# Handing GpSimd's 128x512 and larger work in the first attention to VectorE, and transposing a norm's column without widening it first

## The chip, the cores and the metric

One core of a Trainium2 chip runs the whole program. The metric is the device time of one execution in microseconds. TensorE (PE) does the matmuls, ScalarE (ACT) casts, exponentials and copies, VectorE (DVE) elementwise arithmetic and row maxima, GpSimd (POOL) elementwise arithmetic out of SBUF alone, SyncE (SP) issues the DMAs of the weights. Each engine works through its own queue in order.

## What is computed

A decoder trunk of two layers on 512 tokens of 1024 features, all in float32. The first layer has differential attention with 8 heads (two softmax maps per head, the second subtracted with a factor), the second one latent attention with 8 heads; each is followed by a squared-ReLU MLP. Cut to what matters here:

```python
def rms_norm(x, g, eps=EPS):
    return x * lax.rsqrt(jnp.mean(x * x, axis=-1, keepdims=True) + eps) * g

def apply_rope(x, cos, sin):
    x1, x2 = x[..., :half], x[..., half:]
    return jnp.concatenate([x1 * c - x2 * s, x2 * c + x1 * s], axis=-1)

def diff_attention(hn, ...):
    q, k, v = jnp.split(hn @ w_qkv, ...)
    q, k = apply_rope(q, cos, sin), apply_rope(k, cos, sin)
    s = einsum(q, k) * scale, causal
    p = softmax(s)
    a = p[:, :, 0] - lam * p[:, :, 1]
    o = rms_norm(a @ v, subln_g) * (1 - lambda_init)
    return o @ w_o
...
h = h + diff_attention(rms_norm(h, g0), ...);  h = h + sq_relu_mlp(rms_norm(h, g1))
k_nope, k_rope, v = mla_shared_kv(h, ...)
h = h + mla_attention(rms_norm(h, g2), ...);   h = h + sq_relu_mlp(rms_norm(h, g3))
return rms_norm(h, g_final)
```

## The kernel before

Activations lie with features on the 128 partitions and the 512 tokens along the row. Each float32 product is made of three matmuls on rounded parts (L341 to L353): a value is split into a high part `h`, a cast by ACT, and the rest `l`, a subtraction. For activations the subtraction is VectorE's. For weights, `Weights.prep` (L104 to L115) issues the subtraction (L113) on an engine that is chosen per weight tile; `W_E` is that engine for the weights of both attentions, and `FIRST_E` and `FIRST_BE` choose for the first six and the first four tiles of each. Before, all of the attentions' weight differences but those few are GpSimd's. A weight tile is 128x1024; four raw tiles are loaded ahead, and a raw tile's slot takes its next DMA when its subtraction is done.

`rope` (L485 to L511) rotates a head's queries or keys: ACT copies four swapped blocks of 32 rows from PSUM to `sw` (L492), VectorE multiplies the PSUM row with the cosines into `t` (L499), then `ROPE_E` multiplies `sw` with the sines (L495, called `q0sw` for the queries of head 0) and adds it to `t` (L501, `q0t`). Before, both of these are GpSimd's. Then `stack_q` (L455, L456) or `stack_k` (L470 to L472) make casts on ACT and differences on VectorE: `q0s`, `k0d` and `krest`. The scores of a head need all of them.

The norms' factors are columns: four numbers per partition, one for each 128 tokens. `rsqrt_cols` and L600 make them with a power on GpSimd. Where a factor is needed along the row, `row_wide` (L319 to L323) has VectorE copy the column out to 128x512 (tiles that end in `_w`), and `row_ps` (L325 to L329) has TensorE transpose the four blocks of it into PSUM. This is done for the first norm (the rotation's tables `tac`, `tas` are multiplied by it), for each of the 8 heads of the first attention, and three times ahead of the second (`rbB`, `lq`, `lc`).

The first attention runs tasks of one head and 128 queries: scores into PSUM, masked row maximum on VectorE (`a0..st`), exponential on ACT, the softmax factor `f` (L579, L580), the difference of the two maps (L581), transposes on TensorE, then `ath` (ACT) and `atl` (VectorE, L548), then the product with the values (`a0o`). Other projections fill the time between by a plan of lags (`LAG_A`, `LAG_N`). From the recorded operations a list scheduler puts each engine's instructions in order, by priorities and its own estimates; only at the start and at the very end is the program's order kept.

Of the kernel before, what the change touches and what calls it, by code (L numbers as in the profile page):

```python
# [15 lines left out]
P = 128  # L16
T = 512
NT = T // P
# [207 lines left out]
POOL, DVE = (lambda nc: nc.gpsimd), (lambda nc: nc.vector)  # L226
# [8 lines left out]
AT_C = (29.0, 30.5)  # L235


ROPE_E = (POOL, POOL)
W_E = POOL
FIRST_E = (DVE, DVE, DVE, POOL, DVE, POOL)  # L240
FIRST_BE = (DVE, DVE, DVE, POOL)
LAT_E = (DVE, DVE)


# [10 lines left out]
LAG_N = (2, 2, 4, 1)  # L255
# [6 lines left out]
def trunk(ctx: ExitStack, tc: tile.TileContext, io: dict, out: bass.AP):  # L262
    nc = Engines(tc)
# [10 lines left out]
    def big(name, dt=F32):  # L274
        return ap.tile([P, T], dt, name=name, tag="big", bufs=NBIG)

    def small(name, n=8):
        return ap.tile([P, n], F32, name=name, tag="small", bufs=48)

    def bank(name, tag):  # L280
        return ps.tile([P, T], F32, name=name, tag=tag, bufs=BANKS[tag])
# [33 lines left out]
    def transposes(dst, src_of, n=NT):  # L315
        for i in range(n):
            nc.tensor.transpose(dst[:, i * P:(i + 1) * P], src_of(i), ident)

    def row_wide(cols, name):  # L319
        wide = big(name + "_w")  # L320
        nc.vector.tensor_copy(wide.rearrange("p (i q) -> p i q", q=P),
                              cols.unsqueeze(2).to_broadcast([P, NT, P]))
        return wide  # L323

    def row_ps(wide, name):  # L325

        dst = bank(name + "_ps", "tr")
        transposes(dst, lambda i: wide[:, i * P:(i + 1) * P])
        return dst  # L329

    def split_into(h, l, src, scale=None):
# [8 lines left out]
    def split(src, name, scale=None, tiles=None):  # L340
        h, l = tiles or (big(name + "h", F32R), big(name + "l", F32R))  # L341
        split_into(h, l, src, scale)
        return h, l
# [135 lines left out]
    def mm2(dst, q, k, rest, tok, n, start):  # L479

        nc.tensor.matmul(dst, q[:, tok], k[:, :n], start=start, stop=False)
        nc.tensor.matmul(dst, q[:, tok], rest[:, :n], start=False, stop=True)
        later.spent(2 * PASS * max(256, n))

    def rope(src, tabs, got, name, parts=plain):  # L485
# [8 lines left out]
        def turn():  # L494
            ROPE_E[0](nc).tensor_mul(sw, sw, sinr)  # L495

# [63 lines left out]
    def task_a(hd, i, heads):  # L560

        name, n, tok = hd.name, P * (i + 1), slice(i * P, (i + 1) * P)
        qt = hd.quarter
        weave.need(lambda: len(qt.qs) > hd.hh and len(qt.ks) > hd.hh)
        q, k = qt.qs[hd.hh], qt.ks[hd.hh]
        if i == 0:
            hd.z = small(name + "z", 4)
        z0, z1 = hd.z[:, i:i + 1], small(name + "z1", 1)
        got = []
        for c in range(2):  # L570
            s = bank(f"{name}s{i}{c}", "s")
            mm2(s[:, :n], q[c], k[0][c], k[1][c], tok, n, True)
            got.append(softmax_parts(s, i, SCALE_A, (z0, z1)[c], f"{name}{i}{c}"))
        if i == NT - 1:
            keys_read.add(hd.at)
        yield from wait(LAG_A[1])
        p0, p1 = got
        f = small(name + "f", 1)
        nc.vector.reciprocal(f, z1)  # L579
        nc.vector.tensor_scalar(f, f, z0, nlam, op0=ALU.mult, op1=ALU.mult)  # L580
        nc.vector.scalar_tensor_tensor(p0[:, :n], p1[:, :n], f, p0[:, :n], op0=ALU.mult, op1=ALU.add)  # L581
        yield from wait(LAG_A[2])
        yield from attend(hd, p0, i, LAG_A[3])
        if i < NT - 1:
            return
        yield from wait(LAG_N[0])
        osb = big(name + "osb")
        nc.scalar.copy(osb, hd.o)
        yield from wait(LAG_N[1])
        otok = bank(name + "otok", "tr")  # L590
        transposes(otok, lambda j: osb[:, j * P:(j + 1) * P])
        ss, r = small(name + "ss", 4), small(name + "r", 4)
        junk = big(name + "junk")
        for j in range(NT):
            cols = slice(j * P, (j + 1) * P)
            nc.scalar.activation(junk[:, cols], otok[:, cols], AF.Square, accum_out=ss[:, j:j + 1])
        e = small(name + "e", 4)
        nc.vector.scalar_tensor_tensor(e, hd.z, SUBLN_EPS, hd.z, op0=ALU.mult, op1=ALU.mult)
        nc.vector.scalar_tensor_tensor(e, ss, 1.0 / P, e, op0=ALU.mult, op1=ALU.add)
        nc.gpsimd.tensor_tensor(r, e, mhalf.to_broadcast([P, 4]), op=ALU.pow)  # L600
        yield from wait(LAG_N[2])
        wide = row_wide(r, name + "rb")
        yield from wait(LAG_N[3])
        rbo = row_ps(wide, name + "rb")
        nc.vector.scalar_tensor_tensor(osb, osb, gsub, rbo, op0=ALU.mult, op1=ALU.mult)
        heads[hd.at] = split(osb, name + "on")

# [34 lines left out]
    rt, heads_a, heads_b = [], [None] * NH, [None] * NH  # L642
    r0 = small("r0", 4)
# [19 lines left out]
    ssq_m0, ssq_b, ssq_m1 = [], [], []  # L663
    W.eng = W_E(nc)
    quarters_a = [Quarter() for _ in range(4)]
# [3 lines left out]
    for n in ORDER_A:  # L669
        fill_a += qk_jobs(n) if n < NH else [v_job(n - NH)]  # L670
    for u, e in enumerate(FIRST_E):
        W.specs[u] = W.specs[u][:-1] + (e(nc),)
# [43 lines left out]
    krs, tkq = [], {}  # L716
# [226 lines left out]
    def turn_x(i):  # L943

        tok = slice(i * P, (i + 1) * P)
        trs = [bank(f"xT{i}{n}", "s" if i % 2 else "tr") for n in range(2)]
        for n in range(2):
            transposes(trs[n], lambda c: xt[i][n][:, c * P:(c + 1) * P])
        yield
        tr4 = [t.rearrange("p (c q) -> p c q", q=P) for t in trs]  # L950
        x4 = [big(f"x32{i}{n}").rearrange("p (c q) -> p c q", q=P) for n in range(2)]
        for n in range(2):
            gains = gcol[:, G_ATTN_A + 4 * n:G_ATTN_A + 4 * n + 4]
            nc.vector.tensor_mul(x4[n], tr4[n], gains.unsqueeze(2).to_broadcast([P, 4, P]))
        if i == 0:
            W.prep_h(1)
        else:
            nc.vector.tensor_copy(res[:, 0:4, tok], tr4[0])
        for n in range(2):
            nc.scalar.copy(xa[n][0][:, :, tok], x4[n])  # L960
        if i == 0:
            W.prep(1)
        for n, eng in enumerate((nc.gpsimd, nc.vector) if i == 0 else (nc.vector, nc.gpsimd)):
            h, l = xa[n]
            eng.tensor_sub(l[:, :, tok], x4[n], h[:, :, tok].bitcast(F32))
        if i == 0:
            nc.vector.tensor_copy(res[:, 0:4, tok], tr4[0])
            W.prep(2)
        nc.scalar.copy(res[:, 4:8, tok], tr4[1])
        yield  # L970
# [26 lines left out]
    sum_x(3)  # L997
    fill.pull(v_tile)
    gain_cols(grow_rest, G_ROWS - 16, 16)
    wide = row_wide(r0, "rb0")  # L1000


    lprod = const.tile([P, 2, HD], F32, name="lprod")
# [10 lines left out]
    fill.pull(v_tile)  # L1014
    nc.kept = False
    fill.pull(AT_TABLES)
    rt += tables(row_ps(wide, "rb0"), "ta")
    fill.drain()


# [39 lines left out]
    rB, r2B = small("rB", 4), small("r2B", 4)  # L1060
# [3 lines left out]
    def scale_b():  # L1064
        s = small("bssc", 4)
        col_sums(ssq_b[0], s, "csb")
        rsqrt_cols(rB, s, EPS, 1.0 / D)
        nc.vector.tensor_mul(r2B, rB, rB)
        w = row_wide(rB, "rbB")
        yield  # L1070
        tkq["k"] = tables(row_ps(w, "rbB"), "tk")

    def latent(raw, to, ssq, n, name):

        t, r = small(name + "s", 4), small(name + "r", 4)
        col_sums(ssq[0], t, name + "cs")
        nc.vector.tensor_mul(t, t, r2B)
        rsqrt_cols(r, t, EPS, 1.0 / n)
        nc.vector.tensor_mul(r, r, rB)
        w = row_wide(r, name + "rb")  # L1080
        yield
        row = big(name + "rbs")
        nc.scalar.copy(row, row_ps(w, name + "rb"))
        for m, x in enumerate(raw):
            LAT_E[0](nc).tensor_mul(x, x, row)
            to.append(split(x, f"{name}{m}", tiles=spare_pairs.pop(0) if spare_pairs else None))
# [81 lines left out]
```

## Time and profile before

| | |
|---|---|
| median of 3 runs | 1169.61 us (1167.59 to 1169.77) |
| the profiled execution | 1170.93 us, its span 1169.1 us |
| TensorE busy | 97% |
| VectorE, ACT, GpSimd busy | 53%, 46%, 19% |
| transposed start and first projections | 0 to 38 us |
| first attention | 38 to 260 us |
| first MLP | 260 to 630 us |
| second attention with its projections | 630 to 790 us |
| second MLP, final norm | 790 to 1169 us |

The times are those of one execution, from the start of its span. "Busy" counts an instruction from its start to its end, also where it stands still in between. [...] Waits are read from the view of who waited for whom, by stage.

### The profile page before, as it was taken

What the parts mean: (1) busy time and instruction counts of PE and PEld (TensorE: products, weight loads), DVE (VectorE), ACT (ScalarE), POOL (GpSimd) and SP (SyncE); (2) the same over time, 40 slices, a digit from 0 to 9 for tenths busy, and PEclk for the clock granted to TensorE, in tenths of its full rate; (3) what the DMA queues carried; (4) which work ended last, traced back from release to release, by engine and by line L of the source; (5) the groups of instructions that cost most, each with busy time, mean ns of one, the idle gap of its engine ahead of it and who ended that gap; (6) DMA issues with size and microseconds to landing.
All of it is one profiled execution on the core that took longest, in us unless ns stands there. A gap on an engine that the chain in (4) does not pass through costs nothing.

```text
span 1169.1 us, 14216 instructions
## 1 busy us (share of the span) xinstructions
PE 1137.7 (97%) x5528; PEld 951.8 (81%) x5528; DVE 625.4 (53%) x1035; ACT 541.2 (46%) x984; POOL 217.2 (19%) x144
## 2 busy tenths in 40 slices
PE   7899999999999999999999999999999999999996
PEld 7678888778888888888888789888888888888885
DVE  5677777867643334443555678755444233444232
ACT  6778777655442122442333577635443121443132
POOL 4665544312000100000111242304000000000011
PEclk9899999899999999999999999999999999999999
DMA  7321211213332333333322221123322333332311
GB/s 232 92 72 55 73 55 55 73 37 108 102 96 91 95 103 91 107 91 92 105 92 86 77 72 38 55 71 92 90 91 90 99 100 91 104 94 90 107 56 72
DMA packets 98319, 102.06 MB, mean 87 GB/s; under 512 B 4894, under 2 KB 86476, under 8 KB 98252
## 3 DMA queue, kind: packets, MB, share of 16 engines
q1 hardware_dynamic: 97532, 100.04, 27.8%
q8 instruction: 43, 0.70, 0.3%
q10 hardware_dynamic: 720, 1.11, 0.3%
q14 instruction: 24, 0.20, 0.1%
HBM read 99.05 MB, written 2.10 MB: 87 GB/s over the span
## 4 chain that ended last, share of the span: by engine, by line
PE 82%; ACT 7%; DVE 6%; issue 3%; POOL 1%; DMA 0%; POOLq 0%; SPq 0%; ACTq 0%; DVEq 0%
PE m0d L349 5%; PE m0d L350 5%; PE m0d L348 5%; PE m1u L348 5%; PE m1u L350 5%; PE m0u L348 5%; PE m0u L349 5%; PE m0u L350 5%; PE m1u L349 5%; PE m1d L350 4%; PE m1d L348 4%; PE m1d L349 4%; PE m1d L50 3%; PE ob L348 1%; PE ob L349 1%
## 5 line engine op out<-in xcount | busy, mean ns | idle before, releaser
L854 POOL TENSOR_TENSOR rt<-rt,gfin 128x512 f32<-128x512 f32 x4 | 5.2, 1297 | 301.3 <-ACT fjunk L852 301.1
L348 PE MATMUL m1u<-xn1h,m1u_4h 128*128 128x512 f32 x128 | 50.3, 393 | 0.0
L348 PE MATMUL m1u<-xn0h,m1u_0h 128*128 128x512 f32 x128 | 50.2, 392 | 0.0
L350 PE MATMUL m1u<-xn1h,m1u_4l 128*128 128x512 f32 x128 | 49.9, 390 | 0.0
L350 PE MATMUL m1u<-xn0h,m1u_0l 128*128 128x512 f32 x128 | 49.9, 390 | 0.0
L350 PE MATMUL m0u<-xm1h,m0u_4l 128*128 128x512 f32 x128 | 49.8, 389 | 0.0
L350 PE MATMUL m0u<-xm0h,m0u_0l 128*128 128x512 f32 x128 | 49.8, 389 | 0.0
L349 PE MATMUL m0u<-xm0l,m0u_0h 128*128 128x512 f32 x128 | 49.8, 389 | 0.0
L349 PE MATMUL m0u<-xm1l,m0u_4h 128*128 128x512 f32 x128 | 49.8, 389 | 0.0
L348 PE MATMUL m0u<-xm1h,m0u_4h 128*128 128x512 f32 x128 | 49.8, 389 | 0.0
L349 PE MATMUL m1u<-xn0l,m1u_0h 128*128 128x512 f32 x128 | 49.8, 389 | 0.0
L348 PE MATMUL m0u<-xm0h,m0u_0h 128*128 128x512 f32 x128 | 49.8, 389 | 0.0
L349 PE MATMUL m1u<-xn1l,m1u_4h 128*128 128x512 f32 x128 | 49.8, 389 | 0.0
L365 POOL TENSOR_TENSOR ssq_b<-ssq_b,sq 128x512 f32<-128x512 f32 x7 | 11.7, 1667 | 168.7 <-ACT sq L364 168.7
L695 POOL TENSOR_TENSOR res<-res,m0t 128x512 f32<-128x512 f32 x8 | 10.3, 1290 | 160.7 <-DVE m0t L694 160.7
L113 DVE TENSOR_TENSOR m1u_4l<-m1u_4r,m1u_4h 128x1024 fp32r<-128x1024 f32 x16 | 19.6, 1226 | 36.5 <-ACT m1u_4h L101 36.4
L113 DVE TENSOR_TENSOR m0u_4l<-m0u_4r,m0u_4h 128x1024 fp32r<-128x1024 f32 x16 | 19.9, 1245 | 32.5 <-ACT m0u_4h L101 32.4
L685 DVE TENSOR_TENSOR m1a<-m1u,m1a 128x512 f32<-128x512 f32 x32 | 22.0, 688 | 21.7 <-ACT m1a L684 21.7
L101 ACT CAST m1u_4h<-m1u_4r 128x1024 fp32r<-128x1024 f32 x16 | 16.8, 1050 | 34.7 <-PE m1u L349 21.6
L684 ACT ACTIVATE m0a<-m0u 128x512 f32<-128x512 f32 x32 | 19.0, 594 | 29.7 <-PE m0u L350 29.7
L685 DVE TENSOR_TENSOR m0a<-m0u,m0a 128x512 f32<-128x512 f32 x32 | 22.0, 686 | 19.0 <-ACT m0a L684 19.0
L365 POOL TENSOR_TENSOR ssq_m<-ssq_m,sq 128x512 f32<-128x512 f32 x14 | 20.9, 1494 | 59.0 <-ACT sq L364 58.9
(2301 smaller groups left out, 3720.4 us busy)
## 6 DMA issues: line engine op xcount, KB each, us to landing
m0u_0r<-in_w_up SPq DMA_DIRECT2D x16, 512.0 KB, 3.7
m0u_4r<-in_w_up SPq DMA_DIRECT2D x16, 512.0 KB, 3.7
m1u_0r<-in_w_up SPq DMA_DIRECT2D x16, 512.0 KB, 3.7
m1u_4r<-in_w_up SPq DMA_DIRECT2D x16, 512.0 KB, 3.7
wq_0r<-in_w_qkv_a SPq DMA_DIRECT2D x8, 512.0 KB, 4.9
wk_0r<-in_w_qkv_a SPq DMA_DIRECT2D x8, 512.0 KB, 4.2
xt<-in_x SPq DMA_DIRECT2D x8, 256.0 KB, 5.8
wv_0r<-in_w_qkv_a SPq DMA_DIRECT2D x4, 512.0 KB, 4.5
```

The costliest lines, as they stand in the source:

```text
L50: return self.owner.tc.keep_in_program_order(op(*args, **kw))
L101: self.nc.scalar.copy(d(h), v(self.raws[n]))
L113: eng.tensor_sub(d(to), v(self.raws[n]), d(h).bitcast(F32))
L348: nc.tensor.matmul(dst, ah, bh, start=start, stop=False)
L349: nc.tensor.matmul(dst, ah, bl, start=False, stop=False)
L350: nc.tensor.matmul(dst, al, bh, start=False, stop=stop)
L365: eng(nc).tensor_add(accum, accum, sq)
L684: nc.scalar.activation(a, dst, AF.Relu)
L685: nc.vector.tensor_mul(a, dst, a)
L695: (nc.gpsimd if half == 0 else nc.vector).tensor_add(res[:, c, :], res[:, c, :], t)
L854: nc.gpsimd.tensor_mul(t, t, gfin[0][:, :T])
```

## The change

Four tables change the engine of instructions. `ROPE_E` and `W_E` become VectorE, `FIRST_E` and `FIRST_BE` become empty, and the differences of the input's halves at the start are all VectorE's. `row_wide` goes: the transposes read the column itself with step 0, 128 times per block. GpSimd keeps the small powers and its sums in the MLPs. The lag that stood between the copy and the transposes of a head is kept as one sum.

```diff
-ROPE_E = (POOL, POOL)
-W_E = POOL
-FIRST_E = (DVE, DVE, DVE, POOL, DVE, POOL)
-FIRST_BE = (DVE, DVE, DVE, POOL)
+ROPE_E = (DVE, DVE)
+W_E = DVE
+FIRST_E = ()
+FIRST_BE = ()
...
-    def row_wide(cols, name):
-        wide = big(name + "_w")
-        nc.vector.tensor_copy(wide.rearrange("p (i q) -> p i q", q=P),
-                              cols.unsqueeze(2).to_broadcast([P, NT, P]))
-        return wide
-
-    def row_ps(wide, name):
+    def row_ps(cols, name):
 
         dst = bank(name + "_ps", "tr")
-        transposes(dst, lambda i: wide[:, i * P:(i + 1) * P])
+        transposes(dst, lambda i: cols[:, i:i + 1].to_broadcast([P, P]))
...
-        yield from wait(LAG_N[2])
-        wide = row_wide(r, name + "rb")
-        yield from wait(LAG_N[3])
-        rbo = row_ps(wide, name + "rb")
+        yield from wait(LAG_N[2] + LAG_N[3])
+        rbo = row_ps(r, name + "rb")
...
-        for n, eng in enumerate((nc.gpsimd, nc.vector) if i == 0 else (nc.vector, nc.gpsimd)):
+        for n, eng in enumerate((nc.vector, nc.vector)):
```

The same step from `row_wide` to `row_ps` of the column is made for `r0`, `rB` and the two latents' factors.

VectorE's queue at the keys of head 0, before, from the first product of `k0` to the two differences that its scores need:

```order
L499 TENSOR_TENSOR k0t<-k_0_435,tac 128x512
L456 TENSOR_TENSOR q0s_506<-q0t,q0s_506 64x512
L456 TENSOR_TENSOR q0s_507<-q0t,q0s_507 64x512
L499 TENSOR_TENSOR q1t<-q_0_474,tac 128x512
L472 TENSOR_TENSOR krest_67<-k0t,k0d_552 64x512
L472 TENSOR_TENSOR krest_68<-k0t,k0d_553 64x512
```

VectorE's queue at the same place now, from the sum of the queries' rotation on:

```order
L495 TENSOR_TENSOR q0t<-q0t,q0sw 128x512
L493 TENSOR_TENSOR k0t<-k_0_433,tac 128x512
L113 TENSOR_TENSOR wq_0l<-wq_0r,wq_0h 128x1024
L450 TENSOR_TENSOR q0s_504<-q0t,q0s_504 64x512
L489 TENSOR_TENSOR k0sw<-k0sw,tas 128x512
L450 TENSOR_TENSOR q0s_505<-q0t,q0s_505 64x512
L495 TENSOR_TENSOR k0t<-k0t,k0sw 128x512
L113 TENSOR_TENSOR wk_0l<-wk_0r,wk_0h 128x1024
L493 TENSOR_TENSOR q1t<-q_0_472,tac 128x512
L466 TENSOR_TENSOR krest_67<-k0t,k0d_550 64x512
L489 TENSOR_TENSOR q1sw<-q1sw,tas 128x512
L466 TENSOR_TENSOR krest_68<-k0t,k0d_551 64x512
```

Two weight differences and four rotation steps that were GpSimd's now stand among VectorE's own.

VectorE's queue at the third task of head 0, before, from its second maximum to the `atl` that the next product waits for:

```order
L525 ISA a021sm,a021st<-a0s_738,mask 128x384
L525 ISA a021st 128x1
L548 TENSOR_TENSOR a0atl_724<-a0tr_725,a0ath_723 128x128
L579 RECIPROCAL a0f<-a0z_729 128x1
L580 TENSOR_SCALAR a0f<-a0f,a0z,nlam 128x1
L581 SCALAR_TENSOR_TENSOR a020sm<-a021sm,a0f,a020sm 128x384
L456 TENSOR_TENSOR q2s_751<-q2t,q2s_751 64x512
L456 TENSOR_TENSOR q2s_752<-q2t,q2s_752 64x512
L548 TENSOR_TENSOR a0atl_724<-a0tr_770,a0ath_723 128x2x128
```

VectorE's queue there now:

```order
L519 ISA a021sm,a021st<-a0s_736,mask 128x384
L519 ISA a021st 128x1
L113 TENSOR_TENSOR wq_0l<-wq_0r,wq_0h 128x1024
L542 TENSOR_TENSOR a0atl_722<-a0tr_723,a0ath_721 128x128
L489 TENSOR_TENSOR k2sw<-k2sw,tas 128x512
L573 RECIPROCAL a0f<-a0z_727 128x1
L450 TENSOR_TENSOR q2s_749<-q2t,q2s_749 64x512
L450 TENSOR_TENSOR q2s_750<-q2t,q2s_750 64x512
L574 TENSOR_SCALAR a0f<-a0f,a0z,nlam 128x1
L542 TENSOR_TENSOR a0atl_722<-a0tr_768,a0ath_721 128x2x128
```

A weight difference and a rotation product come ahead of the reciprocal, and the difference of the maps moves behind the `atl`.

VectorE's queue ahead of the second attention, before, where the latent's factor `lcr` is made wide and the latent is scaled (`lat`) and split (`krest`, `lc1l`); `kr` is the rotary key:

```order
L312 TENSOR_SCALAR rs_e<-lcs 128x4
L1079 TENSOR_TENSOR lcr<-lcr,rB 128x4
L113 TENSOR_TENSOR wuq1l<-wuq1r,wuq1h 128x3x256
L321 COPY lcrb_w<-lcr 128x512
L113 TENSOR_TENSOR wuq1l<-wuq1r,wuq1h 128x3x128
L734 TENSOR_TENSOR kr<-kr_ps,krlo 64x512
L499 TENSOR_TENSOR krt<-kr,tkc 128x512
L1085 TENSOR_TENSOR lat_5572<-lat_5572,lcrbs 128x512
L1085 TENSOR_TENSOR lat_5587<-lat_5587,lcrbs 128x512
L335 TENSOR_TENSOR krest_74<-lat_5572,krest_73 128x512
L335 TENSOR_TENSOR lc1l<-lat_5587,lc1h 128x512
```

VectorE's queue there now:

```order
L312 TENSOR_SCALAR rs_e<-lcs 128x4
L726 TENSOR_TENSOR kr<-kr_ps,krlo 64x512
L1069 TENSOR_TENSOR lcr<-lcr,rB 128x4
L113 TENSOR_TENSOR wuq1l<-wuq1r,wuq1h 128x3x256
L113 TENSOR_TENSOR wuq1l<-wuq1r,wuq1h 128x3x128
L493 TENSOR_TENSOR krt<-kr,tkc 128x512
L1074 TENSOR_TENSOR lat_5550<-lat_5550,lcrbs 128x512
L1074 TENSOR_TENSOR lat_5565<-lat_5565,lcrbs 128x512
L489 TENSOR_TENSOR krsw<-krsw,tks 128x512
L329 TENSOR_TENSOR krest_74<-lat_5550,krest_73 128x512
L329 TENSOR_TENSOR lc1l<-lat_5565,lc1h 128x512
```

The copy is gone, the rotary key's sum stands ahead of the latent's factor, and one rotation product stands between scaling and splitting.

## Rows read from the trace of the kernel before

**Rows 1.** The page: busy us, share of the span and instructions by engine.

```profile
PE 1137.7 (97%) x5528; PEld 951.8 (81%) x5528; DVE 625.4 (53%) x1035; ACT 541.2 (46%) x984; POOL 217.2 (19%) x144
```

**Rows 2.** Busy us by stretch: length, engines' busy (instructions), granted clock, DMA share, GB/s.

```profile
60.00:87.00 27.00, 25.30 (x113) 20.76 (x112) 20.18 (x37) 20.89 (x40) 18.74 (x11) 0.94 0.27 78
87.00:224.00 137.00, 129.98 (x824) 115.47 (x823) 107.87 (x267) 109.67 (x273) 69.04 (x40) 0.99 0.20 62
...
700.00:790.00 90.00, 90.00 (x552) 79.80 (x552) 65.56 (x171) 52.24 (x123) 17.18 (x9) 1.00 0.17 54
```

**Rows 3.** Who TensorE waited for, 30 to 87 us: us, times, longest.

```profile
PE a0s L482 <- DVE krest L472: 1.5, 2, 1.2
PE a0s L481 <- ACT k0d L471: 1.5, 2, 1.1
PE a0o L349 <- DVE a0atl L548: 1.1, 1, 1.1
PE a1s L481 <- DVE a030st L525: 0.4, 1, 0.4
```

**Rows 4.** Busy us of three stretches with a low granted clock, columns as rows 2.

```profile
51.40:58.20 6.80, 6.07 (x15) 4.63 (x16) 3.46 (x9) 4.98 (x11) 3.59 (x3) 0.50 0.28 78
82.10:85.50 3.40, 3.31 (x9) 2.73 (x10) 1.76 (x6) 3.31 (x9) 2.55 (x2) 0.50 0.10 29
222.10:228.80 6.70, 6.21 (x18) 4.94 (x18) 3.42 (x13) 2.75 (x12) 1.02 (x1) 0.50 0.15 52
```

**Rows 5.** Timeline from 42 us, GpSimd and VectorE: start, us, instruction, idle before.

```profile
42.65 2.40 POOL L113 TENSOR_TENSOR wq_0l<-wq_0r,wq_0h 128x1024 fp32r<-128x1024 f32 x1
...
43.38 3.92 DVE L456 TENSOR_TENSOR q0s<-q0t,q0s 64x512 fp32r<-64x512 f32 x2 [0.43 <-ACT q0s L455]
...
46.83 1.63 POOL L501 TENSOR_TENSOR k0t<-k0t,k0sw 128x512 f32<-128x512 f32 x1
...
48.42 2.34 POOL L113 TENSOR_TENSOR wk_0l<-wk_0r,wk_0h 128x1024 fp32r<-128x1024 f32 x1
...
49.14 2.17 DVE L472 TENSOR_TENSOR krest<-k0t,k0d 64x512 fp32r<-64x512 f32 x1 [0.96 <-ACT k0d L470]
...
51.61 1.37 DVE L472 TENSOR_TENSOR krest<-k0t,k0d 64x512 fp32r<-64x512 f32 x1 [0.30 <-ACT k0d L470]
```

**Rows 6.** VectorE's groups by shape, 0 to 270 us: count, busy us, mean ns, idle before.

```profile
L472 DVE TENSOR_TENSOR krest<-k7t,k7d 64x512 fp32r<-64x512 f32 x2 | 2.2, 1077 | 0.0
...
L581 DVE SCALAR_TENSOR_TENSOR a100sm<-a101sm,a1f,a100sm 128x128 f32<-128x128 f32 x1 | 1.7, 1693 | 0.0
...
L456 DVE TENSOR_TENSOR q3s<-q3t,q3s 64x512 fp32r<-64x512 f32 x2 | 1.4, 686 | 0.1
...
L113 DVE TENSOR_TENSOR oaw40l<-oaw40r,oaw40h 128x1024 fp32r<-128x1024 f32 x1 | 1.2, 1227 | 0.0
...
L321 DVE COPY a1rb_w<-a1r 128x512 f32<-128x512 f32 x1 | 0.4, 412 | 0.0
```

**Rows 7.** Timeline from 74 us, VectorE and GpSimd, columns as rows 5.

```profile
73.94 0.16 DVE L579 RECIPROCAL a0f<-a0z 128x1 f32<-128x1 f32 x1 [0.91 <-ACT a021sm L527]
...
75.39 4.47 DVE L456 TENSOR_TENSOR q2s<-q2t,q2s 64x512 fp32r<-64x512 f32 x2
...
76.47 2.85 POOL L113 TENSOR_TENSOR wk_0l<-wk_0r,wk_0h 128x1024 fp32r<-128x1024 f32 x1
```

**Rows 8.** Who VectorE waited for, 87 to 224 us, columns as rows 3.

```profile
DVE a1f L579 <- ACT a101sm L527: 1.2, 1, 1.2
```

**Rows 9.** TensorE's weight loads of a transposed tile: count, ns min/median/max, from, to, shape.

```profile
L317 PEld LDWEIGHTS rb_ps<-ident,rb_w x4: 139/140/142, 32.6 to 32.9; 128*128 128x128 f32 x4
```

**Rows 10.** Who TensorE waited for, 224 to 262 us, columns as rows 3.

```profile
PE a7rb_ps L317 <- DVE a7rb_w L321: 1.0, 1, 1.0
```

**Rows 11.** Who TensorE waited for, 650 to 700 us, columns as rows 3.

```profile
PE lcrb_ps L317 <- DVE lcrb_w L321: 0.8, 1, 0.8
PE kn L349 <- DVE lc1l L335: 0.7, 1, 0.7
PE kn L349 <- DVE krest L335: 0.4, 1, 0.4
```

More of the change, by code (lines that the diff above doesn't have):

```diff
@@ L999, in trunk @@
     gain_cols(grow_rest, G_ROWS - 16, 16)
-    wide = row_wide(r0, "rb0")
     lprod = const.tile([P, 2, HD], F32, name="lprod")
@@ L1016, in trunk @@
     fill.pull(AT_TABLES)
-    rt += tables(row_ps(wide, "rb0"), "ta")
+    rt += tables(row_ps(r0, "rb0"), "ta")
     fill.drain()
@@ L1068, in scale_b @@
         nc.vector.tensor_mul(r2B, rB, rB)
-        w = row_wide(rB, "rbB")
         yield
-        tkq["k"] = tables(row_ps(w, "rbB"), "tk")
+        tkq["k"] = tables(row_ps(rB, "rbB"), "tk")
     def latent(raw, to, ssq, n, name):
@@ L1079, in latent @@
         nc.vector.tensor_mul(r, r, rB)
-        w = row_wide(r, name + "rb")
         yield
         row = big(name + "rbs")
-        nc.scalar.copy(row, row_ps(w, name + "rb"))
+        nc.scalar.copy(row, row_ps(r, name + "rb"))
         for m, x in enumerate(raw):
```

## The prediction, made before the change was run

> **What bounds the kernel now.** I read the page first, then the busy time by stage, then who TensorE waits for in the stages that the change touches. TensorE is busy 1137.7 of 1169.1 us [rows 1], so nothing can be won but its waits and its stretches at the low clock. By stage [rows 2]: from 60 to 87 us it has 25.3 of 27.0, from 87 to 224 us 130.0 of 137.0 us, and in the second attention, 700 to 790 us, all of the 90. Nothing of the change lies in the two MLPs.
>
> In the first attention its waits stand in two clusters [rows 3]. At 50 to 53 us it waits 1.5 us for ACT's `k0d` and 1.5 us for VectorE's `krest`: the first head's keys are late. At 80 us it waits 1.1 us for `a0atl` and 0.4 us for the next scores' maximum. [...]
>
> Why the keys are late: the rotation of head 0 runs through GpSimd, and VectorE stands still beside it [rows 5]. VectorE begins the two `q0s` subtractions at 43.38, just inside GpSimd's 2.40 us `wq_0l`, and needs 3.92 us; a pair without GpSimd beside it takes 2 x 0.686 [rows 6]. `krest` begins at 49.14 inside GpSimd's `wk_0l` (48.42 to 50.76) and takes 2.17 us, ending 0.55 us after it. At 75.39 the pair `q2s` takes 4.47 us and ends 0.55 us after GpSimd's `wk_0l`, 76.47 + 2.85 [rows 7]. So a VectorE instruction with both operands in SBUF waits until GpSimd's is over, and then runs.
>
> **The change, part by part.** *Prices.* A 128x1024 weight difference costs GpSimd 2.40 us [rows 5] and VectorE 1.227 [rows 6]. A rotation step of 512 columns cost GpSimd 1.63 (`k0t`, [rows 5]); on VectorE I price it as the differences of 512 columns, 0.69 [rows 6]. The widened copy that goes cost VectorE 0.41 [rows 6].
>
> *Head 0, 38 to 53 us.* VectorE now has q0's product, sum, k0's first product, one weight difference, and so on, in one queue. From `k0t`'s first product to the second `krest` there are 6 rows before and, in the new order, 12 from q0's sum on. The sum of the twelve, at 0.69 each and 1.227 for the two weight differences, is 9.4 us, less what ACT keeps them waiting. I set q0's sum at 39.4: its tables come about 1.1 us earlier, since the 2.5 us `lprod` stall beside GpSimd goes. ACT's casts and half-copies then lie between, and `k0t` is whole at about 45 us instead of 48.46, `krest` at about 49.5 instead of 52.98. TensorE is there at about 48.5 to 49, so of the 3.0 us about 0.7 remain: -2.3 us. With one short wait I expect the clock drop at 51.4 to go as well; in it TensorE was busy 6.07 us at half speed [rows 4], worth -3.0.
>
> *80 us.* Ahead of the late `a0atl` stand now a weight difference and one product, +1.9 us, but the first fills the 0.91 us in which VectorE waited for ACT [rows 7], and the stalls go (4.47 - 2 x 0.686 = 3.1 us in `q2s` [rows 6, 7]), and `a020sm` moves behind. The 1.5 us wait and the 3.4 us at the low clock behind it (3.31 us busy, worth 1.65) would go. VectorE has then to do the whole stretch faster than it ever did, so I count half of 3.1: -1.6.
>
> *87 to 224 us.* VectorE takes over 16 weight differences and 18 rotation steps: 16 x 1.227 + 18 x 0.69 = 32.1 us. It loses the stalls: 21 instructions beside GpSimd took over 0.2 us longer than their like, from `a100sm` (1.693 us) to the last `krest` (mean 1.077 of two) [rows 6], 18.2 us in all, and five copies, 2.1 us. Net +11.8 us on an engine that is busy 107.9 of 137 [rows 2]. The cover: before each softmax factor VectorE waits for ACT's exponential, 17 times, 14.1 us, the first and longest 1.2 [rows 8]; ahead of 12 of these the new order puts a moved instruction, which hides 9.9 us. The other waits for ACT in the stretch (for squares and casts) shrink when VectorE comes later. What is left over is about +1 us, and -0.5 for the wait for `a4rb_w` behind a stall: +0.5. If the cover were gone, all 11.8 would show, since VectorE here hardly ever waits for TensorE.
>
> [...]
>
> *Transposes of the norm's column.* 48 weight loads read one column 128 times. A load from the widened tile takes 139 ns [rows 9]; no row shows one at step 0. Between no change and one load more each (48 x 0.139 = 6.7 us, if nothing hid it) I take zero: it reads as many elements into the same array. A gain I exclude, since TensorE's pace there is set by the matmul. Ends: 0 and +6.7. [...]
>
> *Last head and start.* The 1.0 us before the last head's transposes [rows 10] ended at GpSimd's power, the copy 0.42 of it; the new order brings TensorE there two matmuls earlier, so zero. In the start VectorE gets four differences of 0.69, one of which replaces its own 1.76 us stall; the last lands within 0.2 us of before: zero. No DMA changes its place in SP's queue.
>
> *Second attention.* TensorE waits 0.8 us for `lcrb_w`, 0.7 for `lc1l` and 0.4 for a `krest` [rows 11]. The copy is gone and one weight difference no longer stands between, `kr` moves up before the GpSimd wait, and the `krest` stall (1.62 us instead of 0.69) goes; but TensorE's new order reaches the keys some 1.6 us sooner, so I keep 0.4 of waiting: -1.5. From 700 to 790 us VectorE gets 5 x 1.227 + 4 x 0.69 = 8.9 and loses 4.3 us of stalls, on 65.6 busy of 90 [rows 2]: covered.
>
> **Sum.** -2.3 - 3.0 - 1.6 + 0.5 - 1.5 = -7.9 us. The profiled execution took 1170.93 (span 1169.1), so 1163.0; the median of the runs is 1169.61, 1.3 lower, which gives 1161.7. I say 1162.
>
> **Rivals.** *VectorE becomes the bound from 87 to 224 us.* Place: its queue between two `atl` tiles of one head. For it: 107.9 + 11.8 us in 137, with ACT busy 109.7, and no wait for TensorE left to take slack from. Against: 9.9 us lie in waits that exist. If none of it is covered, +11.8 instead of +0.5 gives -7.9 + 11.3 = +3.4, and clusters of waits pull the clock down once more (+3.0): about 1176. It decides for "slower" when over 8 us of the 11.8 stay uncovered. Chance 0.14.
>
> *The head start is given back.* TensorE leaves 50 us earlier, but VectorE, with 5.6 us net more between 38 and 87 us (20 moved instructions, 17 us, less 11.4 of stalls), isn't ahead by 80; the waits come back one by one, the low clock with them. Then the MLA part and about 1 us are left: 1167.5 to 1169. Chance 0.16.
>
> *More goes than I count.* The waits just before 222 us shrink too, and with them the clock drop there, in which TensorE was busy 6.21 us at half speed [rows 4], worth 3.1; with another 2 us of the waits from 87 us on this gives 1157. Chance 0.15.
>
> *It doesn't do what it says.* The small power instructions stay on GpSimd and stall VectorE as before; under 1 us at each of two heads. This is inside the range.
>
> **How the numbers follow.** Forecast 0.55, the three rivals 0.14, 0.16 and 0.15. The range runs from a little below the third rival to the point where the second has ended and the first begins, with the column's middle price in it: 1155.5 to 1170.5. About 0.2% (2.3 us) is what a measurement of this kernel can tell from no change: faster is the forecast and the third rival, less their tail, 0.69; same the second, 0.17; slower 0.14.
>
> **What would show it.** Right: the clock row stays at 1.0 from 38 to 87 us; `krest` of head 0 takes 0.69 us and ends before 50; no VectorE pair is longer than 0.8 us there; the span to the end of the attention is some 6 us shorter. Wrong: TensorE's waits for `atl` tiles between 87 and 224 us over 10 us in sum, or a weight load of a column above 0.2 us, or 0.5 in the clock row at new places.

## The result and the profile after

The changed kernel takes 1152.7 us (median of 4 runs, 1151.05 to 1153.09) against 1169.56 of the kernel before: the ratio is 0.9857 with a 95% interval of 0.984 to 0.9874. The forecast was 1162 us, 1155.5 to 1170.5. The sign was right, the size was not: 16.9 us went where 7.6 were forecast, and the time lies 2.8 us below the range.

The page of the kernel after, busy us by engine, answers [rows 1]. VectorE is busy for 17 us more, GpSimd for 147 us less, TensorE for 10.6 us less with the same matmuls:

```profile
PE 1127.1 (98%) x5528; PEld 946.1 (82%) x5528; DVE 642.5 (56%) x1104; ACT 540.5 (47%) x984; POOL 69.8 (6%) x63
```

Busy us by stretch, columns as in [rows 2]. From 87 to 224 us VectorE is busy for 120.3 us instead of 107.9, near the 119.7 that the prediction adds up to, and TensorE has 4.3 us more in the same 137 us (the changed kernel is 8 to 16 us further in the program there). The last line is the whole of the span but the cold start and the end: the granted clock is 1.00 throughout, and the three stretches of [rows 4] are gone:

```profile
60.00:87.00 27.00, 26.02 (x134) 21.59 (x133) 24.37 (x59) 24.66 (x52) 0.00 (x0) 1.00 0.26 78
87.00:224.00 137.00, 134.32 (x857) 120.05 (x856) 120.34 (x308) 110.94 (x279) 6.06 (x6) 1.00 0.21 62
...
38.00:1147.00 1109.00, 1097.52 (x5352) 919.48 (x5350) 617.92 (x1060) 517.88 (x939) 64.08 (x49) 1.00 0.27 84
```

Where the time went shows in the starts of some matmuls in the two traces. The middle columns are absolute starts in us, the last two the change from one mark to the next, as measured and as the prediction's terms put it:

| first matmul of | before | after | measured | forecast |
|---|---|---|---|---|
| `a0tr`, head 0's first transposes | 69.82 | 64.86 | -4.96 | -2.3 - 3.0 |
| `a2s`, scores of head 2 | 105.69 | 97.52 | -3.21 | -1.6 |
| `a6s`, scores of head 6 | 197.89 | 185.88 | -3.84 | +0.5 |
| `a7tr`, transposes of head 7 | 232.15 | 215.81 | -4.32 | (in the +0.5) |
| `m0u`, first MLP | 272.55 | 256.09 | -0.12 | 0 |
| `m1u`, second MLP | 805.64 | 787.62 | -1.56 | -1.5 |

The span ends 18.2 us earlier (1169.1 to 1150.9); 0.2 us of that lie behind the last mark. In the first attention the three stretches of [rows 4], in which TensorE's granted clock was 0.50, are gone with 15.59 us of busy time (6.07 + 3.31 + 6.21). What the clock is worth shows in TensorE's starts in the kernel before, at 1.0 and then at 0.50 (start, us, instruction):

```profile
44.03 0.39 PE L349 MATMUL k<-xa0l,wk_0h 128*128 128x512 f32 x1
44.26 0.39 PE L350 MATMUL k<-xa0h,wk_0l 128*128 128x512 f32 x1
...
55.12 0.63 PE L349 MATMUL q<-xa0l,wq_0h 128*128 128x512 f32 x1
55.55 0.63 PE L350 MATMUL q<-xa0h,wq_0l 128*128 128x512 f32 x1
```

A 128x512 matmul starts 0.227 us after the one before it at 1.0 (19 steps from 44.03 to 48.34 us) and 0.427 us at 0.50 (7 steps from 54.70 to 57.69 us). By this pace the 15.59 us do the work of 8.3, and 7.3 us of the gain are the low clock, an estimate from these starts. The expectations below write "at 1.2 GHz" for a granted clock of 0.50; the traces give the clock as a share alone, and what they show at 0.50 is 512 columns in 0.427 us.

TensorE's waits of over 0.2 us between the first scores at 49 us and the first MLP fell from 12.4 to 5.1 us.

### The profile page after: what moved, and what is told of

It is laid out like the page before. It is cut to its first block, busy times and chain, and to the rows that moved or that the text cites. A ratio compares the mean times of both kernels' runs of the same rounds, so it can differ in the third digit from the quotient of the medians.

```text
span 1150.9 us, 14184 instructions
## 1 busy us (share of the span) xinstructions
PE 1127.1 (98%) x5528; PEld 946.1 (82%) x5528; DVE 642.5 (56%) x1104; ACT 540.5 (47%) x984; POOL 69.8 (6%) x63
## 4 chain that ended last, share of the span: by engine, by line
PE 81%; DVE 7%; ACT 6%; DMA 2%; issue 2%; POOL 1%; SPq 0%; POOLq 0%; ACTq 0%; DVEq 0%
PE m0d L343 5%; PE m0d L344 5%; PE m0d L342 5%; PE m1u L342 5%; PE m1u L343 5%; PE m0u L342 5%; PE m1u L344 5%; PE m0u L343 5%; PE m0u L344 5%; PE m1d L342 4%; PE m1d L344 4%; PE m1d L343 4%; PE m1d L50 3%; PE ob L342 1%; PE ob L343 1%
## 5 line engine op out<-in xcount | busy, mean ns | idle before, releaser
L676 ACT ACTIVATE m1a<-m1u 128x512 f32<-128x512 f32 x32 | 19.0, 594 | 27.6 <-PE m1u L344 27.6
L101 ACT CAST m0u_4h<-m0u_4r 128x1024 fp32r<-128x1024 f32 x16 | 16.8, 1052 | 31.5 <-PE m0u L343 25.6
L113 DVE TENSOR_TENSOR m0u_0l<-m0u_0r,m0u_0h 128x1024 fp32r<-128x1024 f32 x16 | 21.0, 1311 | 14.7 <-ACT m0u_0h L101 14.6
```

What stands on the lines that cost most here:

```text
L101: self.nc.scalar.copy(d(h), v(self.raws[n]))
L113: eng.tensor_sub(d(to), v(self.raws[n]), d(h).bitcast(F32))
L676: nc.scalar.activation(a, dst, AF.Relu)
```

## Experiments

Two sums are used below. "Stalls" are what VectorE's instructions between 38 and 224 us took over the usual time of their shape, where that is over 0.2 us: 29.5 us in the kernel before, none in the one after. The shifts are those of the first matmul of the marks above against the kernel before, in us (the last column is the start of the second MLP); the times are medians. A shift is read from one execution of each kernel; the kernel before took between 1166.8 and 1173.0 us in all its runs, so a difference of a microsecond between two rows is not sure.

| kernel | us | stalls | `a0tr` | `a2s` | `a6s` | `a7tr` | `m0u` | `m1u` |
|---|---|---|---|---|---|---|---|---|
| after | 1152.7 | 0 | -5.0 | -8.2 | -12.0 | -16.3 | -16.5 | -18.0 |
| columns alone | 1166.1 | 26.9 | -1.9 | -1.9 | -2.0 | -2.1 | -2.2 | -3.9 |
| rotations alone | 1165.1 | 14.1 | -2.3 | -3.5 | -6.7 | -7.5 | -7.5 | -6.1 |
| weights alone | 1160.7 | 12.0 | -4.3 | -4.3 | -6.7 | -11.2 | -11.3 | -10.0 |
| engines alone | 1158.2 | 0 | -1.7 | -5.0 | -9.1 | -13.4 | -13.4 | -12.8 |
| early heads | 1157.5 | 17.2 | -5.0 | -8.0 | -9.3 | -10.9 | -11.1 | -12.7 |
| late heads | 1162.0 | 13.9 | +0.1 | +0.3 | -2.6 | -6.9 | -7.1 | -8.7 |
| GpSimd beside, all | 1194.6 | 39.1 | +4.4 | +14.9 | +24.4 | +25.4 | +25.3 | +23.7 |
| GpSimd beside, 22 differences | 1177.5 | 26.9 | -1.2 | +3.1 | +8.2 | +8.3 | +8.2 | +6.6 |
| VectorE with 22 more | 1158.0 | 0 | -5.7 | -7.5 | -9.0 | -10.6 | -11.7 | -13.2 |
| halves | 1152.8 | 0 | -4.9 | -8.0 | -12.0 | -16.2 | -16.4 | -17.7 |
| VectorE with 24 more | 1163.9 | 0 | -0.3 | -2.0 | -2.5 | -4.8 | -5.9 | -7.5 |
| GpSimd's copies and fills beside | 1162.7 | 5.1 | +0.6 | -0.7 | -2.6 | -6.2 | -6.3 | -8.0 |

### The parts one by one

Columns alone: the diff of `row_wide` and `row_ps`, with the four tables of before and the start's differences on both engines as before.

> Only the transposes read the norm's column; every engine keeps its work of before. Theory S (the gain comes from VectorE's stalls beside GpSimd's instructions, which go, and from GpSimd's slow rotation, which leaves the path): the stalls stay, the copies of 0.41 us go, so 1166.5 to 1169 us, the three stretches at 1.2 GHz still there. Theory O (the gain comes from the new order of the queues, which the list scheduler makes whatever the engines): a new order alone gives several us, 1163 or less.

Measured: ratio 0.9962 (0.9946 to 0.9978), 3.3 us less. That is below 1166.5 by less than the interval, and the three stretches at granted clock 0.50 are still there (3.4, 3.4 and 6.8 us). Theory O's "several us" don't come. 1.6 of the 3.9 us in the trace are the second attention's.

Rotations alone and weights alone, each a part of the tables with the kernel before:

```diff
-ROPE_E = (POOL, POOL)
+ROPE_E = (DVE, DVE)
```

> The kernel before with the rotations' 16 products and 16 sums of the first attention and those of the second on VectorE, weights' differences on GpSimd as before. Theory S: the rotations caused 5.3 of the 11.4 us of stalls from 38 to 87 us and 6.4 of the 18.1 us from 87 to 224 us; these go, those beside weight differences stay, and the first keys come earlier: 1159 to 1164 us, one or two of the three stretches at 1.2 GHz left. Theory L (only the rotation's latency on GpSimd mattered, twice 1.6 us before each head's scores): nearly the whole gain, 1152 to 1156.

```diff
-W_E = POOL
-FIRST_E = (DVE, DVE, DVE, POOL, DVE, POOL)
-FIRST_BE = (DVE, DVE, DVE, POOL)
+W_E = DVE
+FIRST_E = ()
+FIRST_BE = ()
```

> The kernel before with all weights' differences of both attentions on VectorE, the rotations on GpSimd as before. Theory S: 6.1 us of stalls from 38 to 87 us and 11.7 from 87 to 224 us go; the rotation's latency and its stalls stay: 1159 to 1164 us, the first stretch at 1.2 GHz (51 us) still there. Theory L: little, 1165 to 1168.

Measured: 0.9964 (0.9951 to 0.9977) and 0.9924 (0.9909 to 0.994), 4.3 and 8.7 us less. Rotations alone gave 1 us less than theory S had, weights alone are within it, and theory L falls: the weight differences, which are not in the chain from projection to scores, bring twice as much as the rotations. One expectation was wrong: with weights alone the stretch at 51 us goes too; there is no 0.5 at all up to the end. The three gains add to 16.2 us, against 16.9 of the whole, but not stage by stage: rotations and weights alone each lose 1.3 us or so in the second attention.

Engines alone, the tables and the start's differences with `row_wide` kept:

> The change of engines alone; the norms' columns are still copied wide. If the parts add up: the changed kernel and 3 us, 1155 to 1157, with the second attention's gain of 1.6 us gone (that one is the columns'). If the copies lie in waits that VectorE now has anyway: 1152.5 to 1154.

Measured: 0.9898 (0.9876 to 0.992), 5.5 us over the changed kernel, more than either theory. Here the new queue has a 1.2 us weight difference ahead of the first norm; TensorE waits 2.8 us at 34 us for `va0vl`, and this stretch follows (columns as in [rows 2]):

```profile
36.00:39.40 3.40, 3.40 (x10) 2.65 (x9) 2.97 (x7) 2.05 (x5) 0.00 (x0) 0.50 0.17 50
```

From `a0s`, the first scores, on (+2.7 us against the kernel before, in the changed kernel -0.5) this kernel keeps the gains of the changed one: from `a0tr` to `m0u` both win 11.5 to 11.6 us. So the copies themselves cost nothing in the first attention once VectorE doesn't stall. In the second attention 2.1 us are missing; its gain is the columns'.

### Stall or order

A changed engine also changes the list scheduler's order. This kernel holds the order and brings only GpSimd's work back: the changed kernel, with

```diff
+            if n in self.idle_at:
+                self.nc.gpsimd.tensor_sub(self.raws[n], self.raws[n], h.bitcast(F32))
             self.raws[n] = None
...
+            if name[0] in "qk" and name[1:].isdigit():
+                nc.gpsimd.tensor_mul(sw, sw, sinr)
+                nc.gpsimd.tensor_add(sw, sw, sinr)
```

behind VectorE's own difference and sum. TensorE's queue is that of the changed kernel to the last row; in VectorE's four rows and in ACT's one change places with neighbours.

> The changed kernel; beside its VectorE work GpSimd does again as many instructions of the same sizes as it did before in the first attention (a difference into the raw weight tile after its use, a product and a sum into the rotation's spent tile), with results that nobody reads. The order of every other queue is the same up to a few neighbours. Theory S: the stalls come back, some 29 us from 38 to 224 us, on a VectorE that also has 17 + 32 us more of its own work: 1164 to 1178 us, with waits of TensorE for atl and krest and stretches at 1.2 GHz. Theory O: within 1 us of the changed kernel, 1152 to 1154.

Measured: 1.021 (1.0192 to 1.0229): 41.9 us over the changed kernel, 25 us over the one before, beyond what theory S gave. Theory O falls. Who TensorE waited for most, 38 to 290 us (us, times, longest), and one of five stretches at granted clock 0.50 between 54 and 253 us:

```profile
PE a1tr L320 <- DVE a100sm L583: 5.0, 1, 5.0
PE a0s L479 <- DVE krest L469: 3.7, 2, 2.6
PE a3o L346 <- DVE a3atl L550: 3.6, 1, 3.6
PE a0tr L320 <- DVE a020sm L583: 3.1, 1, 3.1
```

```profile
54.90:61.70 6.80, 3.51 (x9) 2.74 (x10) 5.66 (x8) 3.08 (x8) 5.09 (x4) 0.50 0.27 77
```

In one point this kernel isn't clean: GpSimd's first differences also delay the first norm's power, and `a0s` begins 3.5 us later than in the changed kernel for that. The pair of twins below leaves the first six tiles alone.

### What a microsecond of VectorE costs, plain or stalled

The first kernel for this repeated 24 weight differences on VectorE, `nc.vector` in place of `nc.gpsimd` in the diff above and no rotation:

> The changed kernel; VectorE repeats each of about 24 weight differences of the first attention (1.23 us each, some 29 us), results unread, no GpSimd work beside. This measures what VectorE's time is worth there. Theory V1 (VectorE has waits left, so only what they can't take shows, and a plain microsecond costs less than a stalled one): 5 to 15 us over the changed kernel, 1158 to 1168. Theory V2 (VectorE is now the bound of the stage, so each microsecond shows): 1176 to 1184.

Measured: 1163.9 us, 11.2 over the changed kernel. Theory V2 falls, and the time lies in V1's range, but not all of it is the price that was meant: TensorE waits 4.4 us at 36 us for the first norm, behind the repeats at the start, and `a0s` begins 4.7 us later than in the changed kernel. So two twins with the repeats from the seventh tile on, 22 of them, once VectorE's and once GpSimd's:

```diff
+    W.idle_at = range(6, len(W.specs))
```

> The changed kernel; VectorE repeats the weight differences of the first attention from the seventh tile on (22 of 1.23 us, 27 us), so that the start up to 38 us keeps as it is. Theory T (only VectorE's total time counts, whatever makes it): as much per microsecond as a stall costs in its twin with GpSimd's differences. Theory S (plain time falls into VectorE's waits for ACT, a stall hits what TensorE waits for): 3 to 8 us over the changed kernel, 1156 to 1161, few stretches at 1.2 GHz.

> The twin: the same 22 differences are GpSimd's (2.4 us each, results unread), so VectorE has no more of its own than in the changed kernel, but 22 instructions beside which it stops, by the kernel with all of GpSimd's work beside some 0.9 us each, 20 us in all. Theory T: less than the twin, 2 to 6 us over the changed kernel. Theory S: more than the twin, 10 to 20 us over it, 1163 to 1173, with waits of TensorE behind long VectorE instructions and stretches at 1.2 GHz.

Measured: 0.99 (0.9882 to 0.9919) and 1.0066 (1.0047 to 1.0085): 5.3 and 24.8 us over the changed kernel. Theory T falls: the twin in which VectorE has less of its own work is 19 us slower. Theory S holds, and its 10 to 20 us were too little. TensorE's queue in the GpSimd twin is again that of the changed kernel to the last row. Busy us from 38 to 262 us, first VectorE's 22 more, then GpSimd's:

```profile
38.00:262.00 224.00, 215.80 (x1240) 183.86 (x1239) 206.54 (x450) 171.35 (x401) 17.82 (x13) 1.00 0.21 65
```

```profile
38.00:262.00 224.00, 205.83 (x1150) 177.19 (x1148) 199.32 (x410) 160.98 (x384) 65.07 (x30) 0.95 0.20 60
```

In the first VectorE is busy for 92% of the time and TensorE still does 215.8 us of its work in 224, at 1.00. In the second, busy for 89%, it gets through 410 instructions instead of 450 (22 of these are the repeats), and TensorE does 10 us less, at 0.95. Who TensorE waited for most, 38 to 262 us, in the same order:

```profile
PE a7s L478 <- ACT k7d L468: 1.3, 1, 1.3
PE a1tr L320 <- DVE a0e L597: 1.0, 1, 1.0
```

```profile
PE a3o L346 <- DVE a3atl L547: 3.6, 1, 3.6
PE a0s L479 <- DVE krest L469: 2.6, 2, 2.4
PE a1tr L320 <- DVE a100sm L580: 2.5, 1, 2.5
PE a6tr L320 <- DVE a620sm L580: 2.5, 1, 2.5
```

How such a wait is made, around `a100sm` in the GpSimd twin, VectorE and then GpSimd (start, us, instruction):

```profile
88.78 2.00 DVE L453 TENSOR_TENSOR q4s<-q4t,q4s 64x512 fp32r<-64x512 f32 x1
90.81 2.31 DVE L580 SCALAR_TENSOR_TENSOR a100sm<-a101sm,a1f,a100sm 128x128 f32<-128x128 f32 x1
```

```profile
86.90 3.33 POOL L116 TENSOR_TENSOR wk_0r<-wk_0r,wk_0h 128x1024 f32<-128x1024 f32 x1 [11.71 <-DVE a1f L578]
90.20 2.78 POOL L116 TENSOR_TENSOR wv_0r<-wv_0r,wv_0h 128x1024 f32<-128x1024 f32 x1
```

`q4s` ends 0.55 us after the first GpSimd instruction, `a100sm`, which takes 0.35 us in the changed kernel, 0.14 us after the second. TensorE's transposes wait for it. GpSimd's differences also hold the raw tiles' slots longer, and ACT waits 2.4 us at 58 us and 1.1 us at 170 us, apparently for a late tile; but TensorE has no wait of over 0.25 us in the 17 us behind either, so late weights don't explain its waits. Up to 262 us the stalls are 28.8 us and cost 24.6 at `m0u`: 0.85 us each microsecond. The 22 x 1.22 = 26.8 us of plain work cost 4.8 at `m0u`: 0.18 each. Up to 11.2 us of the difference, by the pace of 0.227 and 0.427 us, are the low clock behind the waits (five stretches, 23.8 us in all at 0.50, in the attention of the GpSimd twin, none in the other). The plain twin's order was made anew by the scheduler, so its price includes what a scheduler that knows of the work can save. Nor is 0.85 a constant: in the two kernels with half of GpSimd's work ("Early or late" below), 17.2 and 13.9 us of stalls stand beside 5.4 and 9.3 us at `m0u` over the changed kernel (2.2 of the 9.3 at `a0s` already), with less work of VectorE's own.

### Which GpSimd instructions

As in the kernel with all of GpSimd's work beside, but a copy in place of the difference, and two fills in place of the product and the sum:

```diff
-                self.nc.gpsimd.tensor_sub(self.raws[n], self.raws[n], h.bitcast(F32))
+                self.nc.gpsimd.tensor_copy(self.raws[n], h.bitcast(F32))
...
-                nc.gpsimd.tensor_mul(sw, sw, sinr)
-                nc.gpsimd.tensor_add(sw, sw, sinr)
+                nc.gpsimd.memset(sw, 0.0)
+                nc.gpsimd.memset(sw, 0.0)
```

> As the kernel with GpSimd's work beside, but GpSimd's instructions are of other kinds: a copy of the weight tile (one operand read) in place of the difference, and two fills (nothing read) in place of the rotation's product and sum. Theory K1 (VectorE stops beside any long GpSimd instruction): waits as with the differences, above 1180 us. Theory K2 (it stops only beside one that reads operands): the copies cost about half of what the differences and rotations cost, 1160 to 1175, and no VectorE instruction is long beside a fill. Theory K3 (only beside two operands): 1152 to 1155.

Measured: 1162.7 us, but 5.6 us of the 10.0 over the changed kernel stand at `a0s`, behind the copies at the start, as above. The rows tell more than the time. No VectorE instruction is long beside one of the 32 fills of 0.53 us; ten are beside copies, 5.1 us up to 224 us. By the rows K2 holds; its price doesn't, as these stalls are an eighth of the 39.1 beside differences and rotations, not half. One place shows both sides, VectorE and then GpSimd:

```profile
88.70 0.68 DVE L453 TENSOR_TENSOR q4s<-q4t,q4s 64x512 fp32r<-64x512 f32 x1
89.41 1.01 DVE L583 SCALAR_TENSOR_TENSOR a100sm<-a101sm,a1f,a100sm 128x128 f32<-128x128 f32 x1
```

```profile
88.73 1.55 POOL L116 COPY wv_0r<-wv_0h 128x1024 f32<-128x1024 f32 x1
```

`q4s` began 0.03 us before the copy and took its usual time; the copy took 1.55 us instead of 1.04. `a100sm` came behind it and ended 0.14 us after it. Of the 22 copies seven took over 1.1 us (1.44 to 2.03), and each of these began at most 0.15 us behind the start of a VectorE instruction with two operands in SBUF; the other 15 took 1.04 or 1.05. So in these rows whichever begins first holds the other up.

### Early or late

The changed kernel with GpSimd's work of before for heads 4 to 7, quarters 2 and 3 and the output projection ("early heads" are VectorE's), and the other half:

```diff
+        there = name[1:].isdigit() and int(name[1:]) not in HEADS_V
+        return nc.gpsimd if there else nc.vector
...
+            W.specs[u] = spec[:-1] + (nc.gpsimd,)
```

> The changed kernel with GpSimd doing again the weight differences and rotations of heads 4 to 7, the values' of quarters 2 and 3 and the output projection's: VectorE has only the early ones. Theory P (each stretch gains what its own stalls cost: about 8.5 us by 95 us, 3.5 from there to 205, 4 around 222, 1.6 in the second attention): 1158 to 1161 us, no stretch at 1.2 GHz before 200 us, one near 215. Theory H (the early keys give TensorE and VectorE a head start from which the later gains follow): 1152 to 1155.

> The other half: GpSimd does again the weight differences and rotations of heads 0 to 3 and the values' of quarters 0 and 1, with the split of the first six tiles as before; the late ones are VectorE's. Theory P: 1169.3 less 3.5, 4, 1.6 and about 1 for the columns: 1159 to 1162 us, the stretches at 1.2 GHz near 51 and 82 us there, the one at 222 not. Theory H: 1164 to 1168.

Measured: 0.9898 (0.9884 to 0.9913) and 0.9937 (0.992 to 0.9954). Theory P holds, the first half 0.5 us better than its numbers; theory H falls. With early heads on VectorE the gain of 8 us at `a2s` is the changed kernel's, and nothing of it is given back later; with late heads alone nothing is gained up to `a2s`, and 7.4 us from there to `m0u`, where the changed kernel has 8.3. Part of the nothing is this kernel's own start: TensorE waits 2.1 us at 33 us for GpSimd's power of the first norm, a stretch at granted clock 0.50 follows that the kernel before doesn't have, and `a0s` comes 1.7 us later than there.

### A candidate for a better version

Halved weight differences from the seventh tile on, and the start's halves on two engines:

```diff
+                if outs is None and not beside and n in self.halved and shape[1] % 2 == 0:
+                    for k in (slice(0, shape[1] // 2), slice(shape[1] // 2, shape[1])):
+                        eng.tensor_sub(l[:, k, :], self.raws[n][:, k, :], h[:, k, :].bitcast(F32))
+                    continue
...
+    W.halved = range(6, len(W.specs))
...
-        for n, eng in enumerate((nc.vector, nc.vector)):
+        for n, eng in enumerate((nc.gpsimd, nc.vector) if i == 0 else (nc.vector, nc.gpsimd)):
```

> A try at a better version: the changed kernel with VectorE's weight differences from the seventh tile on in two halves of 512 columns (so that what TensorE waits for stands behind 0.7 us and not 1.2), and the input's halves at the start on two engines as before. If the waits behind whole differences at 84 us (0.9) and 152 us (1.3) are worth something: 1150 to 1152; if 22 more instructions eat it: 1152 to 1154.

Measured: 1152.8 us, the same as the changed kernel. The wait behind `wv_0l` fell from 1.3 to 0.8 us as meant, but the one of 0.9 us at 84 us stayed, for `a0atl` in place of `a100sm`, and one of 0.4 us came:

```profile
PE a0o L348 <- DVE a0atl L547: 0.9, 1, 0.9
PE a3o L348 <- DVE a3atl L547: 0.8, 1, 0.8
...
PE a1o L347 <- ACT a0osb L587: 0.4, 1, 0.4
```

No version here beats the changed kernel.

## Why the prediction was right in its direction and wrong in its size

**Head 0: right.** -4.96 us measured for -5.3. VectorE's queue in the changed kernel, answering [rows 5]:

```profile
44.23 0.69 DVE L450 TENSOR_TENSOR q0s<-q0t,q0s 64x512 fp32r<-64x512 f32 x1
44.95 0.69 DVE L495 TENSOR_TENSOR k0t<-k0t,k0sw 128x512 f32<-128x512 f32 x1
45.56 1.23 DVE L113 TENSOR_TENSOR wk_0l<-wk_0r,wk_0h 128x1024 fp32r<-128x1024 f32 x1
...
47.40 0.68 DVE L466 TENSOR_TENSOR krest<-k0t,k0d 64x512 fp32r<-64x512 f32 x1
...
49.96 0.69 DVE L466 TENSOR_TENSOR krest<-k0t,k0d 64x512 fp32r<-64x512 f32 x1
```

`k0t` is whole at 45.64 (forecast about 45), each step takes the price that was put on it, the pairs are at 0.69. The second `krest` ends at 50.65, not 49.5, and past the 50 that the prediction had named as a sign. ACT is why: two copies for the next queries stand between the casts.

```profile
47.39 0.62 ACT L465 CAST k0d<-k0t 64x512 fp32r<-64x512 f32 x1
48.03 1.17 ACT L486 COPY q1sw<-q 32x512 f32<-32x512 f32 x2
49.23 0.62 ACT L464 CAST k0d<-k0t 64x512 fp32r<-64x512 f32 x1
```

It cost little, as TensorE came later too; the wait left is 0.7 us, as forecast, and the clock drop went. The -3.0 takes a granted clock of 0.50 as half the work, which no run shows: by the steps of 0.227 and 0.427 us the 6.07 us there are worth 2.8, the 3.31 us at 82 us 1.6 and the 6.21 us at 222 us 2.9.

**80 us: the step that counted half.** The prediction found 3.1 us of wait and low clock there, argued that both would go, and took half. The whole 3.1 went, and a wait of 1.0 us at 93 us with it, which the prediction had left in the next stage; a new one of 0.9 us came, for `a100sm` behind a weight difference. -3.21 is their sum.

**87 to 224 us: the step that failed.** "What is left over is about +1 us, and -0.5 for the wait for `a4rb_w` behind a stall: +0.5". Measured: -3.84 and -4.32 at the two marks. The cover argument held: VectorE was to be 11.8 us busier and is about 12. What failed is the unit. The step balanced VectorE's stalls (18.2 us) against its new work (32.1 us) one to one, as busy time, and of TensorE's waits in this stage it put one into the sum, 0.5 us for `a4rb_w`. The prediction has TensorE's waits "in two clusters", which hold 4.7 us; from 87 to 224 us it waited 6.9 us in the kernel before, in eleven groups, for `atl` tiles, a `krest`, maxima and casts:

```profile
PE a1o L349 <- DVE a1atl L548: 1.0, 1, 1.0
PE a0o L349 <- DVE a0atl L548: 1.0, 1, 1.0
PE a7s L481 <- ACT k7d L471: 1.0, 2, 0.6
PE a7s L482 <- DVE krest L472: 0.7, 1, 0.7
...
PE a4o L349 <- DVE a4atl L548: 0.6, 1, 0.6
PE a4rb_ps L317 <- DVE a4rb_w L321: 0.5, 1, 0.5
```

Ahead of several of these VectorE had stalled: in `a100sm` (1.69 us) before the wait at 93 us, in a `q6s` (1.73) before the one at 185, in `a4rb_w` (1.49) at 212, in a `krest` (1.47) at 222. Of the -3.84, 2.2 us are idle time of TensorE that went and 1.6 us shorter busy time of the same 601 matmuls; of the -4.32, 1.2 us are idle time and 3.1 us shorter busy time (32.07 us at a mean granted clock of 0.90 before, 28.93 at 1.00 after). In the changed kernel, from 78 to 212 us, which is the same part of the program, these are left:

```profile
PE a3o L343 <- DVE a3atl L542: 1.3, 1, 1.3
PE a7s L475 <- ACT k7d L465: 0.9, 2, 0.6
PE a1tr L317 <- DVE a100sm L575: 0.9, 1, 0.9
PE a2tr L317 <- DVE a200sm L575: 0.4, 1, 0.4
```

The twins give an exchange rate for what the step weighed one to one: 0.85 us for a stalled microsecond, 0.18 for a plain one. With these the first attention's 29.5 us of stalls and some 47 us of added work (17.0 + 32.1 - 2.1 in the prediction) make -25.1 + 8.5 = -16.6; -16.45 was measured. This is an estimate after the fact from two other kernels, with a rate for stalls that other pairs of kernels here don't give, and the rotation's own latency isn't in it, so the closeness proves less than it looks.

**The clock at 222 us: in a rival, not in the forecast.** The third rival priced it at 3.1 us and gave it 0.15. It went. Where the wait for head 7's `krest` stays, the drop stays: in the kernel before, with columns alone, and, half as long, with early heads on VectorE, whose waits ahead of it are

```profile
PE a7s L475 <- ACT k7d L465: 1.4, 2, 0.8
...
PE a7s L476 <- DVE krest L466: 0.7, 1, 0.7
```

Where it goes, with weights alone, engines alone, late heads and in the changed kernel, the drop goes. More than this the runs don't show: with rotations alone TensorE waits 3.1 us up to 214 us and 1.0 us at 217, and the clock stays at 1.0; in the GpSimd twin 2.5 us up to 228 come with a drop of 6.8 us. What decides between these is open.

**The other rivals.** "VectorE becomes the bound" needed over 8 of 11.8 us uncovered; the plain twin puts 26.8 us more on top of that and 4.8 show. What costs much here are stalls: 24.6 and 41.8 us at `m0u` with GpSimd's work beside. "The head start is given back" falls with the early heads. "It doesn't do what it says": the powers are still on GpSimd, and none stalls an instruction for over 0.2 us before 224 us.

**The small terms.** Zero for the transposes of a column was right; the row answers [rows 9], a load takes 134 ns where it took 140, and TensorE's four transposes of `a0rb_ps` start 0.11 us apart in both kernels (120.6 to 120.9 us before, 111.7 to 112.0 after):

```profile
L317 PEld LDWEIGHTS rb_ps<-ident,r x4: 133/134/136, 30.0 to 33.4; 128*128 128x128 f32 x4
```

Zero for the start was off by about 0.5 us (the last `rb_ps` transpose ends 0.47 us later). -1.5 for the second attention met -1.6, with another mix: engines alone give back 0.6 us from `m0u` to `m1u`, columns alone win 1.6, so the net gain is the column's. The stall of the `krest` goes with engines alone too, but a new wait of 1.1 us for `vb0vl` comes there.

**The range.** Its low end went with the third rival. The stage from 87 us had no bound below: all of its 6.9 us of waits could go, and with them the low clock behind, the third rival's 3.1. That end lies at 1161.7 - 0.5 - 6.9 - 3.1 = 1151.2.

## What to carry to other kernels

Where two engines hold each other up, count the stalls by who waits behind the stalled instruction, not as busy time of its engine: in one pair of kernels here a microsecond of stall cost 0.85 us, and one of plain work that the scheduler could place cost 0.18. Moving work onto the busier engine can then be the faster way (here VectorE is busy for 17 us more and the time is 16.9 us less). For each stage that a change touches, list what the bounding engine waits for before weighing the busy times, and let the range reach to the end of that list.

## What the hardware showed unexpectedly

- No VectorE instruction is long beside GpSimd's 32 fills of 0.53 us; ten are beside its copies of one operand, by 5.1 us in sum, and a copy that began 0.03 us behind a VectorE instruction took 1.55 us instead of 1.04.
- Not only instructions with both operands in SBUF stall, as the prediction has it: in the kernel before, the copies of one operand `a2rb_w` and `a4rb_w` took 1.64 and 1.49 us instead of 0.41, each begun inside a GpSimd difference and ended 0.3 us after it.
- Waits of 3.1 us (from 210.8 us) and 1.0 us (from 216.3 us) left the granted clock at 1.0 with rotations alone; waits of 0.8, 0.6 and 0.7 us between 210.0 and 213.1 us were followed by 3.4 us at 0.50 with early heads.
- 22 differences on GpSimd whose results nobody reads cost 24.8 us, more than the whole change won (16.9).
